# Branch gates of a hybrid decoder layer: 16 dense units, or seven block products with two of them beside the attention

## The chip, the core and the metric

The kernel runs on one core of one Trainium2 chip. The metric is device time in microseconds, the median of the runs; lower is better. The profile is of one execution, whose span goes from the first to the last instruction.

The engines by their names in the profile: PE is TensorE (matrix products), PEld its weight loads, DVE is VectorE (elementwise), ACT is ScalarE (elementwise, with tables for functions), POOL is GpSimd, SP is SyncE, which here issues every DMA in one queue. An engine works in the order of its own instructions; if one waits, those behind it wait too.

## What is computed

One layer over 1024 tokens of width 2048, in float32. Cut to what matters here:

```python
h = rmsnorm(x, g_pre)
u = h @ w_in                      # q, k, v of two kinds of attention, and two gates of 1024 columns
o_gla = rmsnorm(gla(...), g_gla_head) * silu(g_gate)
o_sb  = stick_breaking(...) * silu(s_gate)
mix = concat([o_gla, o_sb]) @ w_out
x = x + rmsnorm(mix, g_post)
x = x + sigmoid(x @ w_ple_gate + b_ple_gate) * (p @ w_ple_proj)
```

The change is about the 2048 gate columns of `w_in`: silu(g) times the attention's output.

## The kernel before

Everything is held transposed: features on the 128 partitions, tokens along the free dimension in two halves (`HALVES`) of 512. x is 16 tiles of 128 features per half. A float32 product is made of three matmuls in a rounded format: each operand is split (`split`) into `hi`, made by ScalarE, and `lo` = value - hi, made by VectorE, and hi*hi, lo*hi and hi*lo are summed in PSUM. The activations' halves are called `ah` and `al`, the weights' `hi` and `lo` (tiles of 128x512, read into `raw`, two buffers, split into four) or `wh` and `wl` (128x1024, read into `wr`, four buffers, split into three).

The stages, in order:

1. Units. `dense` makes 128 columns of h @ w_in for both halves: four weight tiles of 128x512 (`wload`), 16 x 2 x 3 = 96 matmuls. The 40 units of the attention come first. After each of its 16 steps, `step` lets the attention's generators (`jobs`) go on, so that the attention of one head stands among the units of the next. `rate` says how many pieces of a job one step lets through.
2. Gates. The 16 gate units of 128 columns. The first four (`EARLY_GATES`) are made while the last head's attention runs (`early_gate`), ten behind it from a pool `gates`, and the last two (`LATE_SOLO`), one half at a time, in the stage `mix`. For each gate the sum is multiplied with `rstd` (the norm of x), with its sigmoid and with the attention's output `o`, loaded from `o_d`; the product goes to `og_d`.
3. `w_out`, and after it `w_g` (w_ple_gate), each as a product of 2x2 blocks by 2x2 blocks with seven block products in place of eight (Winograd's form of Strassen's). A block is 512 tokens, 1024 rows and 1024 columns: `product` makes 128 of its columns with 24 matmuls, eight of them (j) one block product. The left factors are blocks and sums of blocks of the activations (A11, A12, A22, S1, S2, S3, S4), which are made and split in the background (`fill`, `sums_12`). The right factors are weight blocks or their sums, made for each j on VectorE (`t1`, `t2`, `t3`, `t4`); `t2` and `t3` go to memory (`t2_d`, `t3_d`) and are loaded again in later stages. `st_u` and `st_v` hold the running sums of the products. `add` and `sub` are lines 772 and 775.

A scheduler orders the instructions of each engine by priorities; `high_priority` (`ahead`, `soon`) moves the weights' loads and splits, and the additions to `u` and `v`, forward. A tile of a pool can only be loaded when what stood in its memory is done with.

In w_out's S2/S1 stage, each j loads three weight tiles, stores two and makes two products, with four `wr` buffers in all. In the code:

```python
b11, t1, t2 = (wload2(w_out[kh, nh, j]) for kh, nh in ((0, 0), (0, 1), (1, 1)))
sub(t1, t1, b11)
sub(t2, t1, t2)
w2, w1 = wsplit(t2), wsplit(t1)
add(b11, b11, t2)
dma(t2_d[j], t2)
dma(t3_d[j], b11)
```

Lines of before named below: 101 every matmul; 112 and 113 the two instructions of `split`; 129 the loads of `raw`; 310 to 331 and 579 to 605 the attention; 701 to 705 an early gate; 720 to 726 a gate of the pool `gates`; 761 the loads into `ar`; 779 the loads into `wr`; 915 the loads of the late gates' weights.

Of the kernel before, what the change touches and what calls it, by code (L numbers as in the profile page):

```python
# [36 lines left out]
def unit_offsets():  # L37
    offs = []
    for h in range(GLA_HEADS):
        offs += [OFF_GK + P * h, OFF_GQ + P * h, OFF_GV + 2 * P * h, OFF_GV + 2 * P * h + P]  # L40
    for h in range(SB_HEADS):
        offs += [OFF_SK + P * h, OFF_SQ + P * h, OFF_SV + P * h]
    offs += [OFF_GG + P * n for n in range(8)]
    offs += [OFF_SG + P * n for n in range(8)]
    return offs


N_UNITS = len(unit_offsets())
GATE0 = 40
EARLY_GATES = 4  # L50
LATE_SOLO = 2
# [8 lines left out]
RATE_BG = 0.5  # L60


@with_exitstack
def layer(ctx, tc, xT, w_in, w_lr, w_a2, b_a, g_pre, g_head, w_out, g_post,
# [15 lines left out]
    w_open = tc.tile_pool(name="w", bufs=4)  # L80
# [81 lines left out]
    urgent, jobs = deque(), deque()  # L162
    rate = [0.0, 0.0]

# [7 lines left out]
    def step():  # L172
        advance(urgent)
        rate[0] += rate[1]
        while rate[0] >= 1.0:
            rate[0] -= 1.0
            advance(jobs)
# [89 lines left out]
    with tc.tile_pool(name="att", bufs=1, reuse_waits="tile") as ap:  # L267
# [395 lines left out]

        rate[1] = RATE_GLA
        heads = [[{}, {}, {}, {}] for _ in range(GLA_HEADS)] + [[{}, {}, {}] for _ in range(SB_HEADS)]
        flat = [(h, i) for h, g in enumerate(heads) for i in range(len(g))]
        for u, (h, i) in enumerate(flat):
# [3 lines left out]
            elif i >= 2:  # L671
                ev = evac_turned(dst, 1 if h < GLA_HEADS else 2)
            else:
                ev = evac_plain(dst)
            if u < 2:
# [21 lines left out]
        def early_gate(n):  # L697
            def go(hf, p):
                gu, ol = at("u"), at("u")
                dma2(ol, part(o_d[hf][n // 2], n))  # L700
                V.tensor_tensor(gu, p, rstd[hf], op=ALU.mult)
                V.tensor_tensor(ol, ol, gu, op=ALU.mult)
                A.activation(gu, gu, AF.Sigmoid)
                V.tensor_tensor(ol, ol, gu, op=ALU.mult)
                dma2(part(og_d[hf][n // 2], n), ol)
            return go

        for n in range(EARLY_GATES):
            dense(U(GATE0 + n), x_act, HALVES, early_gate(n))
        while urgent or jobs:  # L710
            advance(urgent) or advance(jobs)
        own[0].__exit__(None, None, None)

    with tc.tile_pool(name="gates", bufs=1, reuse_waits="tile") as gp:
        def evac_gate(n):
            def go(hf, p):
                gu = gp.tile([P, HT], F32, tag="gu", name=nm("gu"), bufs=2)
                gs = gp.tile([P, HT], F32, tag="gs", name=nm("gs"), bufs=1)
                ol = gp.tile([P, HT], F32, tag="ol", name=nm("ol"), bufs=2)
                dma2(ol, part(o_d[hf][n // 2], n))  # L720
                V.tensor_tensor(gu, p, rstd[hf], op=ALU.mult)
                A.activation(gs, gu, AF.Sigmoid)
                V.tensor_tensor(ol, ol, gu, op=ALU.mult)
                o = gp.tile([P, HT], F32, tag="oB", name=nm("oB"), bufs=1)
                V.tensor_tensor(o, gs, ol, op=ALU.mult)
                dma2(part(og_d[hf][n // 2], n), o)
            return go
# [8 lines left out]

    slots = [[(1, kp) for kp in range(4)], [(1, kp) for kp in range(4, 8)], [(0, kp) for kp in range(4)]]
    with tc.tile_pool(name="mix", bufs=1, reuse_waits="tile") as mp:  # L740
        def mt(tag, bufs, n=W, dt=F32, name=None):
            return mp.tile([P, n], dt, tag=tag, name=nm(name or tag), bufs=bufs)

        for late in (("ev", 2), ("acc", 1), ("sq", 1), ("g", 1, HT), ("pr", 1, 256), ("ph", 1, 256), ("pl", 1, 256),
                     ("ar", 3)):
            mt(*late)
# [12 lines left out]
        def staged(src):  # L759
            t = mt("ar", 3)  # L760
            dma2(t, src)
            return t
# [27 lines left out]
        def product(a, w, mid=None, at=4, p=None, last=True):  # L790
            first = p is None
            p = p or ps("dn")
            hi, lo = w
            for k in range(8):
                sl = slice(k * P, (k + 1) * P)
                ah, al = a[k]
                mm(p, hi[:, sl], ah, first and k == 0, False)
                mm(p, lo[:, sl], ah, False, False)
                mm(p, hi[:, sl], al, False, last and k == 7)
# [15 lines left out]
        def fill(name, slot, make):  # L815
# [6 lines left out]
            sets[name] = parts(pairs)  # L822
# [11 lines left out]
        def sums_12(rows, s1, s2):  # L834
            for i in rows:
                a, b, c = staged(og_d[0][i]), staged(og_d[0][i + 4]), staged(og_d[1][i])
                add(a, a, b)
                sub(c, c, a)
                dma2(s2_d[i], c)
                yield 1  # L840
                s2.append(to_slot(1, i, c))
                yield 1
                if s1 is None:
                    dma2(s1_d[i], a)
                else:
                    s1.append(to_slot(2, i, a))
                yield 1

        def last_sums(s2):
            s1 = []  # L850
            for i in range(3):
                s1.append(to_slot(2, i, staged(s1_d[i])))
                yield 1
            yield from sums_12((3,), s1, s2)
# [4 lines left out]

        s1_d = drams("s1_d", 3)  # L860
# [43 lines left out]
        early = []  # L904
        for hf in (1, 0):
            if hf == 0:
                job(fill("A11", 0, plain(og_d[1])))
                job(sums_12(range(3), None, early))
            for n in range(KT - LATE_SOLO, KT):
                p = None  # L910
                for kh in HALVES:
                    with ahead():
                        raw = mt("wr", 4)
                        for q in range(2):
                            dma(part(raw, q), w_in[GATE0 + n, 2 * kh + q])
                        w = wsplit(raw)
                    p = product(x_act[hf][8 * kh:8 * kh + 8], w, p=p, last=kh == 1)
                with soon():
                    if n % 2 == 0:
                        z = mt("ev", 2)  # L920
                    V.tensor_tensor(part(z, n), p, rstd[hf], op=ALU.mult)
                    if n % 2:
                        o, g = staged(o_d[hf][n // 2]), mt("sq", 1)
                        A.activation(g, z, AF.Sigmoid)
                        V.tensor_tensor(z, z, o, op=ALU.mult)
                        V.tensor_tensor(z, z, g, op=ALU.mult)
                        dma2(og_d[hf][n // 2], z)
        drain()

        job(last_sums(early))  # L930
# [10 lines left out]
        job(fill("S3", 0, both(og_d[0], og_d[1], sub)))  # L941
        for j in range(8):
            with ahead():
# [5 lines left out]
                dma(t2_d[j], t2)  # L949
                dma(t3_d[j], b11)  # L950
# [8 lines left out]
        job(fill("A22", 1, plain(og_d[0][4:])))  # L959
        job(fill("A12", 2, plain(og_d[1][4:])))  # L960
        for j in range(8):
# [3 lines left out]
            with soon():  # L965
                if j % 2 == 0:
                    c = mt("ev", 2)
                add(part(c, j), p, v(j))
                add(u(j), p, u(j))
                if j % 2:  # L970
                    dma2(c_d[0][4 + j // 2], c)
# [252 lines left out]
```

## Time and profile before

| | us |
|---|---|
| median of 3 runs | 2149.65 (2147.41 to 2150.99) |
| the profiled execution | 2148.85 |
| its span | 2147.1 |
| TensorE's mean granted clock | 0.994 |
| stretch with four gates beside the last attention | 1078 to 1185 |
| ten gates alone | 1185 to 1412 |
| last two gates, then w_out and w_g | from 1423 |

All DMA moved 300 MB. A group row of the profile gives the line, engine and operation, the tiles written and read, the shape and the count, then busy time in us and the mean of one in ns, then the idle time of the engine just ahead of them and what ended it (`<-`). A row of the timeline gives start, duration, engine and the same names; in brackets the idle time ahead. The rows come in the prediction, where they are used.

### The profile page before, as it was taken

The page shows a single profiled execution, that of the slowest core. Times are in us where ns is not written, and L with a number is a line of the kernel's source. Part 1 is how long each engine was busy: PE and PEld are TensorE (multiplying, and loading weights), DVE is VectorE, ACT ScalarE, POOL GpSimd, SP SyncE. Part 2 cuts the span into 40 slices and gives each one's busy share as a digit, 9 for nine tenths or more (in the row PEclk, how much of TensorE's full clock was granted, in tenths as well). Part 3 has the DMA queues.
Part 4 walks back from the last instruction along what each step waited for, and adds up shares of the span by engine and source line. Part 5 has one row for each costly group of instructions (what it writes and reads, how often), then busy time and mean ns, then how long its engine had stood idle before and what let it go on. Part 6 is the DMA issues. An engine that isn't in the chain of part 4 may idle for free.

```text
span 2147.1 us, 26863 instructions
## 1 busy us (share of the span) xinstructions
PE 2111.7 (98%) x9904; PEld 1746.6 (81%) x9904; DVE 1372.7 (64%) x2147; ACT 831.1 (39%) x1347; POOL 106.7 (5%) x228
## 2 busy tenths in 40 slices
PE   9999999999999999999999999979999999999998
PEld 6788888888888888888888888868788888778787
DVE  8557676766666666666666232336777787886665
ACT  7333333333455454544544111123233443432332
POOL 3000000000101110110110000000000000000000
PEclk9999999999999999999999999989999999999999
DMA  6222221222233333333334333258887686786663
GB/s 205 73 54 56 59 61 59 55 60 55 62 86 89 75 89 88 89 81 78 93 102 120 94 98 98 87 174 311 312 319 251 219 312 205 271 286 219 223 206 123
DMA packets 215844, 300.38 MB, mean 140 GB/s; under 512 B 122913, under 2 KB 127905, under 8 KB 215713
## 3 DMA queue, kind: packets, MB, share of 16 engines
q1 hardware_dynamic: 215712, 298.67, 44.5%
q8 instruction: 77, 1.26, 0.2%
q14 instruction: 55, 0.44, 0.1%
HBM read 215.25 MB, written 56.10 MB: 126 GB/s over the span
## 4 chain that ended last, share of the span: by engine, by line
PE 77%; DMA 10%; DVE 8%; issue 2%; ACT 2%; SPq 0%; DVEq 0%; POOL 0%; ACTq 0%
PE dn L101 67%; PE z L101 5%; DMA wr<-w_g 3%; PE t L101 2%; PE o L101 2%; DVE wl L113 2%; DMA E<-X 1%; DMA ar<-h_d 1%; DMA ar<-og_d 1%; DMA wr<-w_out 1%; DVE ev L772 1%; DVE al L113 1%; DVE wr L772 1%; ACT ah L112 0%; DMA ar<-c_d 0%
## 5 line engine op out<-in xcount | busy, mean ns | idle before, releaser
L101 PE MATMUL dn<-ah,hi 128*128 128x512 f32 x1728 | 686.2, 397 | 0.2 <-ACT u L679 0.2
L101 PE MATMUL dn<-al,hi 128*128 128x512 f32 x1728 | 674.4, 390 | 0.9 <-DVE al L238 0.9
L101 PE MATMUL dn<-ah,lo 128*128 128x512 f32 x1728 | 673.8, 390 | 0.0
L101 PE MATMUL dn<-ah,wh 128*128 128x512 f32 x960 | 375.6, 391 | 11.0 <-ACT wh L112 11.0
L101 PEld LDWEIGHTS dn<-ah,hi 128*128 128x128 f32 x1728 | 325.0, 188 | 71.5 <-issue 3.6
L101 PEld LDWEIGHTS dn<-al,hi 128*128 128x128 f32 x1728 | 324.3, 188 | 72.2 <-DVE al L238 2.6
L101 PE MATMUL dn<-ah,wl 128*128 128x512 f32 x960 | 375.4, 391 | 3.5 <-DVE wl L113 3.5
L101 PE MATMUL dn<-al,wh 128*128 128x512 f32 x960 | 374.7, 391 | 0.0
L101 PEld LDWEIGHTS dn<-ah,lo 128*128 128x128 f32 x1728 | 325.2, 188 | 60.1
L112 ACT ACTIVATE hi<-raw 128x512 fp32r<-128x512 f32 x216 | 135.6, 628 | 304.5 <-PE dn L101 301.8
L113 DVE TENSOR_TENSOR lo<-raw,hi 128x512 fp32r<-128x512 f32 x216 | 150.3, 697 | 154.9 <-ACT hi L112 154.4
L101 PEld LDWEIGHTS dn<-ah,wh 128*128 128x128 f32 x960 | 181.4, 189 | 49.8 <-ACT wh L112 11.5
L101 PEld LDWEIGHTS dn<-ah,wl 128*128 128x128 f32 x960 | 181.5, 189 | 42.3 <-DVE wl L113 4.5
L101 PEld LDWEIGHTS dn<-al,wh 128*128 128x128 f32 x960 | 181.0, 189 | 37.5
L112 ACT ACTIVATE wh<-wr 128x1024 fp32r<-128x1024 f32 x120 | 126.0, 1055 | 186.7 <-PE dn L101 116.4
L113 DVE TENSOR_TENSOR wl<-wr,wh 128x1024 fp32r<-128x1024 f32 x120 | 145.8, 1218 | 18.3 <-ACT wh L112 17.8
L320 ACT ACTIVATE X<-E 128x256 uint16<-128x256 uint16 (+2 forms) x96 | 81.0, 844 | 128.5 <-DVE E L595 117.2
L590 DVE TENSOR_TENSOR_SCAN X<-X 128x128 f32<-128x128 f32 (+2 forms) x96 | 98.1, 1021 | 37.1 <-POOL X L584 24.6
L605 DVE COPY v<-E 128x512 uint16<-128x512 uint16 (+1 forms) x160 | 63.6, 430 | 59.5 <-DMA E<-X 50.2
L112 ACT ACTIVATE ah<-ar 128x1024 fp32r<-128x1024 f32 x48 | 50.9, 1061 | 105.8 <-DVE ar L775 50.8
L113 DVE TENSOR_TENSOR s<-v,s 128x512 fp32r<-128x512 f32 (+1 forms) x82 | 52.3, 637 | 48.3 <-ACT s L112 46.4
L112 ACT ACTIVATE s<-v 128x512 fp32r<-128x512 f32 (+1 forms) x82 | 47.9, 584 | 74.6 <-DVE v L605 43.3
(208 smaller groups left out, 2178.3 us busy)
## 6 DMA issues: line engine op xcount, KB each, us to landing
raw<-w_in SPq DMA_DIRECT2D x216, 256.0 KB, 2.7
wr<-w_g SPq DMA_DIRECT2D x64, 512.0 KB, 4.4
wr<-w_out SPq DMA_DIRECT2D x56, 512.0 KB, 4.8
ar<-og_d SPq DMA_DIRECT2D x36, 512.0 KB, 5.4
ar<-h_d SPq DMA_DIRECT2D x36, 512.0 KB, 4.8
xraw<-xT SPq DMA_DIRECT2D x32, 256.0 KB, 4.4
o_d<-o SPq DMA_DIRECT2D x32, 256.0 KB, 2.0
t_d<-wr SPq DMA_DIRECT2D x16, 512.0 KB, 3.2
```

What stands on the lines that cost most here:

```text
L101: PE.matmul(o, lhsT, rhs, start=start, stop=stop)
L112: A.activation(hi, src, AF.Copy)
L113: (eng or V).tensor_tensor(lo, src, f(hi), op=ALU.subtract)
L320: A.activation(pl.rearrange("p (two n) -> p two n", two=2), src.bitcast(U16)[:, :2 * n].rearrange("p (n two) -> p two n", two=2), AF.Copy)
L590: V.tensor_tensor_scan(rev, rev, rev, initial=kq[:, n:n + 1], op0=ALU.mult, op1=ALU.bypass)
L605: V.tensor_copy(to[:, :, :m, j], w[:, :, 2 * g:2 * g + m])
L772: V.tensor_tensor(dst, a, b, op=ALU.add)
```

## The change

The gates are made as the later two products are, by seven block products: the left factor is x times g_pre (not yet times `rstd`, which is multiplied in at the end), the right one `w_gate`, the gate columns as 2x2 blocks.

- `x_sums` makes the four sums S1 to S4 of x's blocks during the attention, from x in memory, 128x512 at a time in `u` tiles, and stores them (`sx_d`). It goes on once in 15 steps, and in the tail (from the first gate product on) `x_set` loads and splits S2 and S1 once in 4.
- Two block products, A11 by B11 and A12 by B21, are made by `small_product` beside the last attention, from `raw` tiles of 128x512: eight (j) of the first, whose results go to memory (`u1_d`, evacuated by ScalarE), and eight of the second, added to the first: gates 0 to 7 of the first half (`gate_11`). The last four of these (`LAST_11`) stand behind the attention and use the pool `mix`, which is opened ahead of them; the weights' pool is on the other side of the memory and stays open. The pool `gates` is gone.
- In the stage `mix`, S2/S1, A22, S3 and S4 follow as in the other two products; the gates of the second half come out in the S3 stage, the rest of the first half in the S4 stage (`gate`, two units at a time).
- `w_out` and `w_g` are made with the halves of the tokens exchanged: w_out's first product now takes og of the first half. `sums_12` makes S1 and S2 of w_out beside that product and splits both there; before, three of the four S1 tiles were stored and loaded again.
- `ar` has four buffers and not three, `ev` four and not two. The products of the per-layer embedding (`embed`) take turns on three PSUM tags.

The diff, cut:

```diff
-        for n in range(EARLY_GATES):
-            dense(U(GATE0 + n), x_act, HALVES, early_gate(n))
-        while urgent or jobs:
+        def small_product(a, src, evac):
+            p = ps("dn")
+            for q in range(2):
+                hi, lo = wload(part(src, q))
+                for kk in range(4):
+                    k = 4 * q + kk
+                    sl = slice(kk * P, (kk + 1) * P)
+                    ah, al = a[k]
+                    mm(p, hi[:, sl], ah, k == 0, False)
+                    mm(p, lo[:, sl], ah, False, False)
+                    mm(p, hi[:, sl], al, False, k == 7)
+                    if k % 2:
+                        step()
+            with tc.high_priority(offset=300):
+                evac(p)
+        def gate_11(j, new):
+            def go(p):
+                gu, ol = new(), new()
+                dma2(gu, part(u1_d[j // 2], j))
+                dma2(ol, part(o_d[0][j // 2], j))
+                V.tensor_tensor(gu, p, gu, op=ALU.add)
+                V.tensor_tensor(gu, gu, rstd[0], op=ALU.mult)
+                V.tensor_tensor(ol, ol, gu, op=ALU.mult)
+                A.activation(gu, gu, AF.Sigmoid)
+                V.tensor_tensor(ol, ol, gu, op=ALU.mult)
+                dma2(part(og_d[0][j // 2], j), ol)
+            return go
+        while beside:
+            advance(beside)
+        rate[1], pace[1] = RATE_TAIL, PACE_TAIL
+        beside.append(x_set("S2", 1))
+        for j in range(8):
+            small_product(x_act[0][:8], w_gate[0, 0, j], keep_u1(j))
+        while beside:
+            advance(beside)
+        beside.append(x_set("S1", 0))
+        for j in range(8 - LAST_11):
+            small_product(x_act[0][8:], w_gate[1, 0, j], gate_11(j, lambda: at("u")))
+        while urgent or jobs or beside:
...
-    with tc.tile_pool(name="gates", bufs=1, reuse_waits="tile") as gp:
...
-        for n in range(EARLY_GATES, KT - LATE_SOLO):
-            dense(U(GATE0 + n), x_act, HALVES, evac_gate(n))
+    for j in range(8 - LAST_11, 8):
+        small_product(x_act[0][8:], w_gate[1, 0, j], gate_11(j, lambda: part(mt("ar", 4), 0)))
...
-            for n in range(KT - LATE_SOLO, KT):
...
+        t2_d, t3_d = drams("g2_d", 8), drams("g3_d", 8)
+        for i in range(4):
+            dma2(st_u[i], u1_d[i])
+        for j in range(8):
+            with ahead():
+                b11, t1, t2 = (wload2(w_gate[kh, nh, j]) for kh, nh in ((0, 0), (0, 1), (1, 1)))
+                sub(t1, t1, b11)
+                sub(t2, t1, t2)
+                w2, w1 = wsplit(t2), wsplit(t1)
+                add(b11, b11, t2)
+                dma2(t2_d[j], t2)
+                dma2(t3_d[j], b11)
+            p = product(g_sets["S2"], w2)
+            with soon():
+                add(u(j), p, u(j))
+            p = product(g_sets["S1"], w1)
+            with soon():
+                add(v(j), p, u(j))
+        drain()
...
+            p = product(sets["S3"], w)
+            gate(j, 1, p, u(j))
+            gate(8 + j, 1, p, v(j))
...
+            p = product(sets["S4"], w)
+            gate(8 + j, 0, p, v(j))
...
+        job(sums_12())
```

Two places of the engines' orders. First VectorE beside the last attention. Before, among an early gate's rows (`lo` is a weight's split, `u` at lines 702 and 704 the gate, `v`, `s`, `X`, `E`, `eb` the attention):

```order
L113 TENSOR_TENSOR lo_10685<-raw_10683,hi_10684 128x512
L702 TENSOR_TENSOR u_10461<-u_10461,u_10460 128x512
L702 TENSOR_TENSOR u_10469<-u_10469,u_10468 128x512
L605 COPY v_10553<-E_2183_10415 128x2x2x128
L704 TENSOR_TENSOR u_10461<-u_10461,u_10460 128x512
L704 TENSOR_TENSOR u_10469<-u_10469,u_10468 128x512
L590 SCALAR_TENSOR_TENSOR X_10500<-X_10500 128x128
L113 TENSOR_TENSOR s_2216_10557<-v_10553,s_10556 128x512
L594 COPY eb_10510<-X_10500 128x1
L595 TENSOR_TENSOR E_10501<-E_10501,X_10500 128x128
```

Of the change, in the middle of the first block product (`al` is the split of a part of S2; a weight's split is line 112 now, the attention's rows are 593 to 608):

```order
L112 TENSOR_TENSOR al_10538<-u_10453,ah_10537 128x512
L608 COPY v_10606<-E_2199_10475 128x2x2x128
L112 TENSOR_TENSOR lo_10686<-raw_10684,hi_10685 128x512
L112 TENSOR_TENSOR s_2231_10610<-v_10606,s_10609 128x384
L112 TENSOR_TENSOR al_10538<-u_10541,ah_10537 128x512
L593 SCALAR_TENSOR_TENSOR X_10566<-X_10566 128x384
L112 TENSOR_TENSOR st_10658<-u_10132,st_10658 128x128
L598 TENSOR_TENSOR E_10567<-E_10567,X_10566 128x384
L112 TENSOR_TENSOR al_10727<-u_10633,ah_10726 128x512
L112 TENSOR_TENSOR lo_10745<-raw_10743,hi_10744 128x512
```

Between the attention's rows now stand splits of weights and of S2. From one weight split (`lo`) to the next are eight rows here; before they are fifteen.

Second SP's queue where the large weight tiles begin. Before, behind the last gates (`ol` is the attention's output, `oB` a finished gate):

```order
L720 DMA ol_12586<-o_d_0_687 128x512
L726 DMA og_d_1_711<-oB_12459 128x512
L720 DMA ol_12596<-o_d_1_695 128x512
L726 DMA og_d_0_703<-oB_12591 128x512
L726 DMA og_d_1_711<-oB_12601 128x512
L915 DMA wr_12684<-w_in 128x512 x2
L915 DMA wr_12716<-w_in 128x512 x2
```

Of the change (line 745 loads parts of S1, 786 stores a gate, 635 the attention's last output, 851 is `wload2`):

```order
L128 DMA raw_11483<-w_gate 128x512
L786 DMA og_d_0_702<-u_11283 128x512
L635 DMA o_d_1_700<-o_11335 128x512
L128 DMA raw_11501<-w_gate 128x512
L786 DMA og_d_0_702<-u_11352 128x512
L128 DMA raw_11530<-w_gate 128x512
L851 DMA wr_11664<-w_gate 128x1024
L128 DMA raw_11548<-w_gate 128x512
L851 DMA wr_11666<-w_gate 128x1024
L851 DMA wr_11668<-w_gate 128x1024
```

The first wr tile was loaded behind the last gate's store; now it is asked for ahead of the last raw tile, among the last four small products.

More of the change, by code (lines that the diff above doesn't have):

```diff
@@ L731, in layer @@
-    w_open.__exit__(None, None, None)
[L739 to L746, printed above, removed]
+    mp = ctx.enter_context(tc.tile_pool(name="mix", bufs=1, reuse_waits="tile"))
@@ L901, in stream @@
             yield 1
[L904 to L908, printed above, removed]
-            for n in range(KT - LATE_SOLO, KT):
[L910 to L927, printed above, removed]
@@ new lines, in layer @@
+        drain()
+        job(fill("S3", 1, plain(sx_d["S3"])))
+        job(fill("S4", 2, plain(sx_d["S4"])))
+        for j in range(8):
+            with ahead():
+                t4, t2 = wload2(w_gate[1, 0, j]), wload2(t2_d[j])
+                add(t4, t4, t2)
+                w = wsplit(t4)
+            p = product(x_act[1][8:], w)
+            with soon():
+                add(u(j), p, u(j))
+        drain()
+        for j in range(8):
+            with ahead():
+                w = wsplit(wload2(t3_d[j]))
+            p = product(sets["S3"], w)
+            gate(j, 1, p, u(j))
+            gate(8 + j, 1, p, v(j))
@@ L931, in layer @@
+        drain()
+        job(fill("A11", 0, plain(og_d[0])))
+        for j in range(8):
+            with ahead():
+                w = wsplit(wload2(w_gate[1, 1, j]))
+            p = product(sets["S4"], w)
+            gate(8 + j, 0, p, v(j))
+        drain()
+        st_u, st_v = state("h"), state("l")
+        job(sums_12())
         for j in range(8):
```

238 lines of the change are left out of this document (143 added, 95 removed).

## The prediction

> **What bounds the kernel now.** I read the page first, then TensorE's waits behind the attention, then the windows and the timeline around the gates. On the page TensorE is the engine without spare time:
>
> ```profile
> PE 2111.7 (98%) x9904; PEld 1746.6 (81%) x9904; DVE 1372.7 (64%) x2147; ACT 831.1 (39%) x1347; POOL 106.7 (5%) x228
> L101 PE MATMUL dn<-ah,hi 128*128 128x512 f32 x1728 | 686.2, 397 | 0.2 <-ACT u L679 0.2
> ```
>
> The 397 ns of one matmul is not what a matmul costs, since they overlap. What it costs is seen where nothing else runs, in the dense stretch of the chain of work behind the attention (start, us, what):
>
> ```profile
> 1184.90 226.48 PE dn L101 x999
> ```
>
> 226.48 us / 999 = **0.2267 us** per 128x512 matmul; a matmul that goes is worth this and not 0.397. The Trainium skill says the same in "Perfetto Trace Analysis", section "Identifying the Most-Contended Engine": busy time of matmuls is no measure of their cost. By busy time 192 matmuls would be 192 x 0.397 = 76 us; by the chain they are 43.5 us, and the sum goes by the chain.
>
> Where TensorE waits from the gates to the end of the kernel (who <- whom: us, times, longest):
>
> ```profile
> PE dn L101 <- ACT wh L112: 11.0, 1, 11.0
> PE z L101 <- DVE ev L1060: 4.2, 1, 4.2
> PE z L101 <- DVE pl L113: 3.6, 3, 1.8
> PE dn L101 <- DVE wl L113: 3.5, 2, 3.1
> ```
>
> The one wait of 11.0 us is at the end of the gates:
>
> ```profile
> 1411.66 0.39 PE L101 MATMUL dn<-al,hi 128*128 128x512 f32 x1
> ...
> 1416.67 0.69 DVE L725 TENSOR_TENSOR oB<-gs,ol 128x512 f32<-128x512 f32 x1 [2.10 <-DMA og_d<-oB]
> 1417.76 10.80 SPq L915 DMA_DIRECT2D wr<-w_in  x14
> 1421.97 1.06 ACT L112 ACTIVATE wh<-wr 128x1024 fp32r<-128x1024 f32 x1 [6.73 <-DMA wr<-w_in]
> ...
> 1423.08 0.80 PE L101 MATMUL dn<-ah,wh 128*128 128x512 f32 x1 [11.04 <-ACT wh L112]
> ...
> 1427.92 0.57 PE L101 MATMUL dn<-ah,wh 128*128 128x512 f32 x1
> ...
> 1428.33 0.39 PE L101 MATMUL dn<-ah,wl 128*128 128x512 f32 x1
> ```
>
> The first weights of the last stage are only asked for (SPq) when the last gate is written, because they stand in memory that the gates' pool held. Ten matmuls then start 0.43 us apart, at a lower granted clock. From 1411.66 to 1428.33 eleven steps take 16.67 us instead of 11 x 0.2267 = 2.49: **14.2 us** lost.
>
> **What is removed.** The gates were 16 units x 2 halves x 48 = 1536 matmuls; seven block products are 7 x 8 x 24 = 1344. The 192 that go are 192 x 0.2267 = **-43.5 us**. All of them are 128x512, and TensorE's order ahead of the gates stays, but for a few places where attention rows stand one step earlier or later.
>
> The gates' pool goes, and w_gate's first wr loads stand in SP's order ahead of the last raw load, among the last small products. The load after which they come waits for a split, which waits for a weight buffer that comes free 84 matmuls (19 us) before the first product with wr. From issue to landing such a load takes 4.8 us (page, part 6):
>
> ```profile
> wr<-w_out SPq DMA_DIRECT2D x56, 512.0 KB, 4.8
> ```
>
> With two differences and a split that is 4.8 + 2 x 1.22 + 1.06 + 1.22 = 9.5 us (VectorE's rows below, ScalarE's 1.06 above). So it should be hidden; bounds 0 and 14.2, I take 2 left over: **-14.2 + 2 us**.
>
> A third, smaller loss stands in w_out's S2/S1 stage:
>
> ```profile
> 1250.00:1300.00 50.00, 50.00 (x222) 41.38 (x222) 14.06 (x22) 8.00 (x13) 0.00 (x0) 1.00 0.27 90
> 1500.00:1550.00 50.00, 46.92 (x200) 38.15 (x199) 37.46 (x35) 15.78 (x18) 0.00 (x0) 0.97 0.89 316
> 1530.19 0.50 PE L101 MATMUL dn<-ah,wl 128*128 128x512 f32 x1 [3.08 <-DVE wl L113]
> ```
>
> (Columns of a window: us; busy and count of PE, PEld, DVE, ACT, POOL; clock; DMA share; GB/s.) 22 matmuls too few are 5.0 us: 3.1 of waiting, the rest lower clock behind it. Part of the cause goes, since S1 is no longer written to memory and loaded again there, but the four wr buffers with three loads and two stores per j stay. Bounds 0 and -5.0; I take **-2.5 us**.
>
> **What is added: VectorE beside the attention.** This term decides the size. In the stretch in which four gates run beside the last attention now:
>
> ```profile
> 1078.00:1184.90 106.90, 106.90 (x524) 90.48 (x523) 66.84 (x123) 47.77 (x90) 9.54 (x24) 1.00 0.39 109
> ```
>
> TensorE is never idle and VectorE is busy 66.84 of 106.90 us (0.625). What of it is gates and weights, and which of its waits are which (the groups of this window; last columns: busy, mean ns, idle before):
>
> ```profile
> L113 DVE TENSOR_TENSOR lo<-raw,hi 128x512 fp32r<-128x512 f32 x17 | 11.7, 686 | 12.1 <-ACT hi L112 12.1
> L605 DVE COPY v<-E 128x512 uint16<-128x512 uint16 x21 | 9.1, 458 | 5.2 <-DMA E<-X 4.9
> L113 DVE TENSOR_TENSOR s<-v,s 128x512 fp32r<-128x512 f32 x9 | 6.2, 686 | 7.8 <-ACT s L112 7.8
> L702 DVE TENSOR_TENSOR u<-u,u 128x512 f32<-128x512 f32 x6 | 4.0, 685 | 2.9 <-DMA u<-o_d 2.9
> L701 DVE TENSOR_TENSOR u<-dn,rstd 128x512 f32<-128x512 f32 x6 | 4.0, 683 | 1.8 <-PE dn L101 1.8
> L113 DVE TENSOR_TENSOR s<-v,s 128x384 fp32r<-128x384 f32 x5 | 2.8, 557 | 1.8 <-ACT s L112 1.7
> L704 DVE TENSOR_TENSOR u<-u,u 128x512 f32<-128x512 f32 x6 | 3.9, 683 | 0.0
> ```
>
> The attention itself is 66.84 - 11.7 - 4.0 - 4.0 - 3.9 = 43.2 us of VectorE, and 106.9 - 392 x 0.2267 = 18.0 us of TensorE (392 of the 524 are dn). The other prices:
>
> ```profile
> L113 DVE TENSOR_TENSOR lo<-raw,hi 128x512 fp32r<-128x512 f32 x216 | 150.3, 697 | 154.9 <-ACT hi L112 154.4
> L113 DVE TENSOR_TENSOR wl<-wr,wh 128x1024 fp32r<-128x1024 f32 x120 | 145.8, 1218 | 18.3 <-ACT wh L112 17.8
> L772 DVE TENSOR_TENSOR wr<-wr,wr 128x1024 f32<-128x1024 f32 x32 | 39.2, 1224 | 46.5 <-DMA wr<-w_g 32.9 <-DMA wr<-t_d 7.4 <-issue 6.0
> L897 DVE SCALAR_TENSOR_TENSOR ar<-ar,c,rstd 128x512 f32<-128x512 f32 x16 | 11.5, 746 | 7.0 <-DMA ar<-c_d 7.0
> ```
>
> A small product uses a split weight for one half of the tokens and not for two, so its splits are twice as dense. Twelve of them beside the attention: TensorE 288 x 0.2267 + 18.0 = 83.3 us. VectorE 43.2 + 24 splits x 0.697 + 16 splits of S2 and S1 x 0.697 + four gates x 4 x 0.684 = 43.2 + 16.7 + 11.2 + 10.9 = 82.0 us. The four late products with the first pair of weights: TensorE 96 x 0.2267 = 21.8; VectorE 8 x 0.697 + 10.9 + 3 x 1.224 + 2 x 1.218 = 22.6. Together **104.6 us of VectorE under 105.1 us of TensorE**. VectorE works in its order, so each wait in that order now moves TensorE, which waits for lo and s. It cannot gain: TensorE has no idle time there to give. The bounds are 0 and all of VectorE's waits in the window that do not come from its lead on weights: 106.9 - 66.84 - 12.1 = 28 us. I take the part which stays when VectorE is late: a copy v, ScalarE's split of it and the difference s follow each other closely, 7.8 + 1.8 = 9.6 us: **+10 us**.
>
> Behind them a pair j of the gates' S2/S1 stage costs VectorE 3 x 1.224 + 2 x 1.218 + 2 x 0.684 = 7.5 of TensorE's 10.9 us, so it gets its lead back. But the stage is built as w_out's, with four wr buffers, and starts without a lead: I take the 5.0 us that w_out's costs (bounds 0 and 10): **+5 us**.
>
> **What I cost at nothing.** S1 to S4 of x: 32 VectorE instructions, about 24 x 0.746 + 8 x 0.684 = 23.4 us over a thousand us, with 16 ACT copies. The attention has room:
>
> ```profile
> 1050.00:1100.00 50.00, 50.00 (x246) 42.26 (x245) 30.54 (x56) 25.47 (x45) 2.09 (x8) 1.00 0.33 85
> ```
>
> Without the cover it is 23 us at most. Its 64 transfers on SP stand between raw loads; a wait of theirs for a u buffer holds the raw loads behind it, which lead by four buffers of 24 matmuls. The gates' other stages: S3 costs VectorE 1.218 + 2 x 0.684 + 3 x 1.22 = 6.2 us per j against TensorE's 5.4, 6 us over in all, which three weight buffers (16 us) carry until S4, where it is 4.3. Exchanging the halves later changes names, not counts.
>
> **The sum**, against the profiled execution: 2147.1 - 43.5 - 14.2 + 2 - 2.5 + 10 + 5 = 2103.9 us of span; this execution took 1.75 us more than its span (2148.85), so 2105.7. The median of the runs shown, 2149.65, is 0.8 above it; I leave that out: **2106 us**.
>
> **The rivals.**
> *All is hidden.* VectorE reaches a full window in w_out's S2/S1 stage, so its waits could vanish (here us, busy VectorE, clock, DMA share, GB/s):
>
> ```profile
> 1540.00:1550.00 10.00, 10.00 (x11) 1.00 0.86 310
> ```
>
> No +10, +5, +2, and all 5.0 gained: 2147.1 - 43.5 - 14.2 - 5.0 + 1.75 = 2086. Against it speaks that the s chain is in the order itself. Chance 0.13.
>
> *DMA becomes the bound.* The new stages move, per 43.5 us, 24 transfers of 0.524 MB = 12.6 MB (A22: 16 loads of weights, 8 of S3 and S4; S3: 8 weights, 8 o, 8 og; w_out's first: 8 weights, 8 og, 8 stores), and 50 MB in the two double stages: 289 GB/s over some 350 us, S4 less. Now:
>
> ```profile
> 1450.00:1500.00 50.00, 50.00 (x223) 41.39 (x222) 30.50 (x28) 17.26 (x20) 0.00 (x0) 1.00 0.88 313
> 1550.00:1600.00 50.00, 50.00 (x223) 41.39 (x222) 39.58 (x39) 15.53 (x16) 0.00 (x0) 1.00 0.86 310
> ```
>
> 310 GB/s ran without a wait, which speaks against it; the 5.0 us at 316 GB/s for it. With one such loss in each of six stages: 2147.1 - 43.5 - 14.2 - 5.0 + 2 + 10 + 30 + 1.75 = 2128. Chance 0.12.
>
> *Slower: VectorE keeps its old share beside the attention.* If its waits grow with its work and it stays at 0.625, the 104.6 us take 167, 62 over TensorE's 105.1: 2105.7 - 10 + 62 = 2158. It decides below a share of 104.6 / (105.1 + 57) = 0.645 (over 2154). Against it: many of its present waits are lead, as the 12.1 us before lo. Chance 0.05, and 0.03 for a time beside no change.
>
> *The clock.* The 3.08 us wait above cost 5.0 us in all. If the 10 us come as three such waits they cost three times 1.9 more: 2111, inside the forecast. The Trainium skill, "TensorE: Matmul & The Clock Gate", section "What's actually happening", puts the idle window that halves the clock at about 3.4 us, by which waits of 3 us would cost nothing more; the 0.43 us steps behind this shorter wait say otherwise.
>
> **Chances.** Forecast 0.67 (own range 2094 to 2122), all hidden 0.13, DMA 0.12, slower 0.05, no change 0.03. The range of 8 in 10 goes from the hidden case to the DMA case with the late end of the tail's bound: 2086 to 2132. A measurement of this kernel tells about 0.2% from no change: faster 0.92, same 0.03, slower 0.05.
>
> **What would show it.** 9712 matmul records instead of 9904; the 11.0 us wait gone, with wr<-w_gate issued before the last small product; VectorE near 0.9 in the hundred us around the end of the attention, with TensorE waiting there for lo, s or wl. Wrong would be: no idle TensorE there (then 2086 to 2096), waits on wr from DMA all through the gates (then 2128), or VectorE under 0.65 (then slower).

## The result, and the profile after

| | before | after |
|---|---|---|
| median | 2148.53 us (4 runs, 2146.87 to 2150.99) | 2123.07 us (4 runs, 2120.21 to 2126.72) |
| profiled execution | 2148.85 | 2120.21 |
| its span | 2147.1 | 2118.3 |
| all DMA | 300 MB | 354 MB |

The ratio is 0.9882, 95% interval 0.9862 to 0.9901: faster, by 25 us (1.2%) and not by the 43 that were forecast. 2123 lies in the range of 2086 to 2132.

The engines' row on the page of after (lines are those of after: 100 is every matmul, 111 and 112 the split):

```profile
PE 2077.2 (98%) x9712; PEld 1712.5 (81%) x9712; DVE 1504.3 (71%) x2271; ACT 876.0 (41%) x1393; POOL 106.0 (5%) x228
```

9712 matmuls: the 192 are gone. The wait of 11.0 us for `wh` is gone too. In its place stand 13.3 us in four waits of TensorE for VectorE to take results out of PSUM (TensorE's waits from 1185 us on; who, for whom: us, times, longest):

```profile
PE dn L100 <- DVE ar L781: 8.2, 3, 4.8
PE dn L100 <- DVE st L844: 5.2, 1, 5.2
...
PE dn L100 <- DVE wl L112: 0.7, 1, 0.7
```

Line 781 is the addition in `gate_11` and 844 is `add`. Both read a `dn` bank of PSUM, and what waits is a matmul that wants that bank. Waiting for weights (`wl`) is down to 0.7 us.

To see where the time went I cut both executions at the same instructions. The last attention is cut from one of its value products on, which stands at 1092.42 us before and at 1095.47 us after:

```profile
1092.42 0.80 PE L101 MATMUL t<-s,u 128*128 128x256 f32 x6
```

```profile
1095.47 0.69 PE L100 MATMUL t<-s,u 128*128 128x256 f32 x5
```

From there to the end of the attention (us; busy and count of PE, PEld, DVE, ACT, POOL; clock; DMA share; GB/s), before:

```profile
1092.42:1184.90 92.48, 92.48 (x452) 78.23 (x451) 59.13 (x109) 42.87 (x81) 9.54 (x24) 1.00 0.41 114
```

and after, with the stretch behind it and the place of w_out's S2/S1 stage:

```profile
1095.47:1186.40 90.93, 83.30 (x392) 67.66 (x391) 64.62 (x119) 54.83 (x106) 8.81 (x23) 0.98 0.72 192
1186.40:1330.00 143.60, 130.27 (x548) 106.17 (x547) 101.66 (x111) 40.22 (x48) 0.00 (x0) 0.95 0.81 285
1500.00:1550.00 50.00, 49.25 (x217) 40.46 (x217) 37.55 (x37) 11.23 (x11) 0.00 (x0) 1.00 0.88 328
```

- Ahead of the cut: 3.05 us later than before.
- Beside the attention: 60 matmuls fewer are 13.6 us, but the stretch is only 1.55 us shorter. **12.0 us** are lost. VectorE is busy for 64.62 of 90.93 us, a share of 0.71.
- From the attention's end to 1330: 548 matmuls are 124.2 us of 143.6. **19.4 us** are lost, where before lost 14.2 at the end of its gates.
- w_out's S2/S1 stage: 5 matmuls too few in place of 22, so 1.1 us in place of 5.0.

-43.5 + 3.05 + 12.0 + 19.4 - 14.2 - 3.9 = -27.2 us, where the spans differ by -28.8; the other 1.6 us are spread over later stages.

The 19.4 us, row by row. These rows are picked from the timeline of after around the first products of the gates' S2/S1 stage; `...` parts one wait from the next (779 is a late gate's load of u1, 112 on `wl` the split of the weights, 998 the stores of `t3`, 989 the loads of u1 into `st_u`):

```profile
1202.18 0.43 SPq L779 DMA_DIRECT2D ar<-u_d  x1
1209.49 2.35 DVE L112 TENSOR_TENSOR wl<-wr,wh 128x1024 fp32r<-128x1024 f32 x2
1211.77 0.69 DVE L781 TENSOR_TENSOR ar<-dn,ar 128x512 f32<-128x512 f32 x1
1212.60 0.76 PE L100 MATMUL dn<-ah,wh 128*128 128x512 f32 x1 [3.10 <-DVE ar L781]
...
1230.81 0.32 SPq L998 DMA_DIRECT2D g_d<-wr  x1
1231.22 0.41 SPq L779 DMA_DIRECT2D ar<-u_d  x1
1235.10 0.69 DVE L781 TENSOR_TENSOR ar<-dn,ar 128x512 f32<-128x512 f32 x1 [0.81 <-DMA ar<-u_d]
1235.94 0.60 PE L100 MATMUL dn<-ah,wh 128*128 128x512 f32 x1 [4.84 <-DVE ar L781]
...
1242.99 0.32 SPq L998 DMA_DIRECT2D g_d<-wr  x1
1243.41 0.40 SPq L989 DMA_DIRECT2D st<-u_d  x1
1248.37 0.77 PE L100 MATMUL dn<-ah,wh 128*128 128x512 f32 x1 [5.15 <-DVE st L844]
```

The four `dn` banks hold the last gates' products, and each is free when line 781 has read it. Two things make that late. For the first of these gates it is VectorE's order: its u1 was asked for at 1202.18 and had landed 6.7 us later, but its addition stands behind the weight sums and two splits, which end at 1211.8, and VectorE is not idle ahead of it. TensorE waits 3.10 us. For the last gate it is the load of u1: SP issues it (1231.22) only behind a store that waits for VectorE's weight sum, and VectorE then stands 0.81 us until it has landed. TensorE waits 4.84 us. Such a load is the cause at 1243.41 too: the first loads for the S2 products' additions go out behind the stores of a later pair of weights, 31 us after the stage's first matmul (1212.60). This reading is a theory so far. Its rival is the one that the prediction had: weights without a lead.

### The profile page after: what moved, and what is told of

It reads as the page before. It is cut to its first block, busy times and chain, and to the rows that moved or that the text cites. A ratio compares the mean times of both kernels' runs of the same rounds, so it can differ in the third digit from the quotient of the medians.

```text
span 2118.3 us, 26833 instructions
## 1 busy us (share of the span) xinstructions
PE 2077.2 (98%) x9712; PEld 1712.5 (81%) x9712; DVE 1504.3 (71%) x2271; ACT 876.0 (41%) x1393; POOL 106.0 (5%) x228
## 4 chain that ended last, share of the span: by engine, by line
PE 73%; DMA 11%; DVE 10%; issue 3%; ACT 3%; SPq 0%; POOL 0%; DVEq 0%; ACTq 0%; POOLq 0%
PE dn L100 63%; PE z L100 5%; PE t L100 2%; PE o L100 2%; DVE wl L112 2%; DMA wr<-w_g 2%; DMA E<-X 1%; DMA ar<-og_d 1%; DMA wr<-w_gate 1%; DVE ev L844 1%; DMA wr<-w_out 1%; DMA ar<-h_d 1%; DMA xraw<-xT 1%; DVE al L112 1%; DVE wr L844 1%
## 5 line engine op out<-in xcount | busy, mean ns | idle before, releaser
L100 PE MATMUL dn<-ah,hi 128*128 128x512 f32 x1408 | 562.1, 399 | 0.2 <-ACT u L716 0.2
L100 PE MATMUL dn<-ah,lo 128*128 128x512 f32 x1408 | 549.9, 391 | 0.6 <-DVE lo L112 0.6
L100 PE MATMUL dn<-al,hi 128*128 128x512 f32 x1408 | 550.0, 391 | 0.4 <-DVE al L241 0.3
L100 PE MATMUL dn<-ah,wh 128*128 128x512 f32 x1216 | 476.0, 391 | 13.3 <-DVE ar L781 8.2
L100 PE MATMUL dn<-ah,wl 128*128 128x512 f32 x1216 | 475.6, 391 | 0.7 <-DVE wl L112 0.7
L100 PE MATMUL dn<-al,wh 128*128 128x512 f32 x1216 | 475.1, 391 | 0.1
L100 PEld LDWEIGHTS dn<-ah,hi 128*128 128x128 f32 x1408 | 265.3, 188 | 59.2 <-issue 2.8
L100 PEld LDWEIGHTS dn<-al,hi 128*128 128x128 f32 x1408 | 264.5, 188 | 59.0 <-DVE al L241 1.9
L100 PEld LDWEIGHTS dn<-ah,lo 128*128 128x128 f32 x1408 | 265.4, 189 | 48.7 <-DVE lo L112 1.1
L844 DVE TENSOR_TENSOR st<-dn,st 128x512 f32<-128x512 f32 x88 | 60.1, 686 | 47.7 <-PE dn L100 46.8
```

Of the source, the lines that this page charges most:

```text
L100: PE.matmul(o, lhsT, rhs, start=start, stop=stop)
L844: V.tensor_tensor(dst, a, b, op=ALU.add)
```

## The experiments

Each ran beside the kernel before on its own chip; ratios are to that.

**1. x_sums alone.** The kernel before, with `x_sums` and its steps and nothing else of the change.

```diff
+        pace[0] += 1
+        if pace[0] % pace[1] == 0:
+            advance(beside)
...
+            if u == 5:
+                beside.append(x_sums())
```

> The kernel before with the sums S1 to S4 of x made and stored during the attention and used by nobody (everything else as before, so the output is unchanged). The trace of the change enters the last attention 3.05 us later than before. If the sums cause that, this kernel is 3 us slower than before (2150 to 2154), with the loss ahead of 1095 us. If the prediction's price holds (hidden), it is within 1 us of before. If their VectorE time were exposed in full, it would be 23 us slower.

Measured: 2150.4 us against 2146.92, ratio 1.0017 (1.0005 to 1.0028). The last head's first 128x128 score product, before:

```profile
1097.23 0.22 PE L101 MATMUL z<-b,st 128*128 128x128 f32 x1
```

and here:

```profile
1102.94 0.22 PE L101 MATMUL z<-b,st 128*128 128x128 f32 x1
```

From there to the attention's end both take the same, 87.67 and 87.66 us. So the sums cost 5.7 us ahead of this point in this order, where the changed kernel was 3.05 us late: not nothing, and far from 23. Over the whole kernel they cost 3.5 us by the medians, as the first theory had it; in these two executions 2.4 us come back behind the attention.

**2. The last four gates' products leave PSUM by ScalarE.** `late_act`: a copy first, which needs no load, then the addition from the copy.

```diff
+    def gate_freed(j):
+        def go(p):
+            t, g = part(freed[j // 2 % 2], j), mt("ar", 4)
+            A.activation(t, p, AF.Copy)
+            gate_11(j, iter((part(g, 0), part(g, 1))).__next__)(t)
+        return go
...
-        small_product(x_act[0][8:], w_gate[1, 0, j], gate_11(j, lambda: part(mt("ar", 4), 0)))
+        small_product(x_act[0][8:], w_gate[1, 0, j], gate_freed(j))
```

> The last four gates' products are copied out of PSUM by ScalarE at once, so that no PSUM bank waits for VectorE's addition or for the load of u1; all else as in the change, four 0.6 us copies more on ScalarE. Theory PSUM (the late additions hold the four banks and TensorE stands still for them): the waits of 3.1, 0.2 and 4.8 us and the slow clock behind them go, 10 to 16 us faster than the change (about 2109). Theory lead (the first wr tile is asked for only 9.6 us ahead of the last small product's end, and four wr buffers give a pair of weights only every 10.5 to 12 us): TensorE then waits for wh or wl at nearly the same times, 0 to 4 us faster (2119 to 2123).

Measured: 2117.6 us, ratio 0.9868 (0.9851 to 0.9884). The waits for line 781 are gone, and one wait takes their place (853 is `add` here, 1007 a store of `t3`, 998 the loads of u1 into `st_u`, 112 the split of the third pair's first weights):

```profile
1229.55 1.23 DVE L112 TENSOR_TENSOR wl<-wr,wh 128x1024 fp32r<-128x1024 f32 x1
...
1240.50 0.32 SPq L1007 DMA_DIRECT2D g_d<-wr  x1
1240.92 0.40 SPq L998 DMA_DIRECT2D st<-u_d  x1
...
1245.46 1.89 DVE L853 TENSOR_TENSOR st<-dn,st 128x512 f32<-128x512 f32 x3 [1.82 <-DMA st<-u_d]
1246.30 0.76 PE L100 MATMUL dn<-ah,wh 128*128 128x512 f32 x1 [14.61 <-DVE st L853]
```

TensorE made products until all four banks were full and then stood for 14.61 us, until the load issued at 1240.92 let VectorE add. Banks, not weights, stop it: the fifth product needs the first weights of the third pair, and these were split by 1230.78 us, before the fourth product's last matmul (1231.31). The loss to 1330 is 17.6 us. The time, 5.5 us under the change, is what neither theory had forecast: the waits for line 781 went, as the theory of PSUM said, but the wait for line 844 grew by 9.5 us.

**3. Six late gates.** `last6`: more work between the attention and the stage.

```diff
-LAST_11 = 4
+LAST_11 = 6
```

> Six of the second product's eight parts stand behind the attention and not four (LAST_11 = 6), so 29 matmuls (6.6 us) more lie between the attention's end and the first S2 product. Theory lead: wr is asked for as much earlier, and the loss between the attention's end and 100 us behind it falls from 19 to about 12 us. Theory PSUM: six late additions hold the banks, the loss stays at 19 or grows. Beside the attention ten products stand and not twelve; if VectorE and the attention's own pace set the time there, that stretch gets shorter by less than the matmuls moved out of it, and its loss grows from 11 to 13 to 17 us, so that the total stays within 4 us of the change.

Measured: 2116.38 us, ratio 0.9858 (0.9843 to 0.9872). The first wr load goes out at 1186.62 us, 13 us earlier than in after, and still there is one wait of 9.38 us for line 781; the loss to 1330 is 12.1 us. The 12.1 us are what the theory of the lead had forecast, and the time, 6.7 us under the change, is more than the 4 us of the other. But the mechanism is not the lead's: no wait for `wh` or `wl` stands there in either kernel, and with a lead longer by 13 us the wait for a bank stays, longer than any in after. It is now a late gate's own product that waits, for an addition that stands in VectorE's order behind the second pair's weight sums. Why the loss as a whole fell, this run alone does not tell.

**4. The loads of u1 early.** `st_first`: the four loads into `st_u` get a higher priority and stand in SP's order right behind the first pair's stores. `banks` is this and the copies of 2 together.

```diff
-        for i in range(4):
-            dma2(st_u[i], u1_d[i])
+        with tc.high_priority(offset=1500):
+            for i in range(4):
+                dma2(st_u[i], u1_d[i])
```

> The early loads of u1 alone, beside the changed kernel's own order of additions. If PSUM banks set it: only the wait for the S2/S1 products' additions goes (5.15 us in the changed kernel), the waits for the last four gates' additions (3.1 + 0.2 + 4.8 us) stay; loss 13 to 16 us in place of 19.4, 2116 to 2120 us. If the lead of the weights sets it: loss 18 us or more, 2121 to 2124 us.

> The last four gates' products are copied out of PSUM by ScalarE, and the four loads of u1 that the first S2 and S1 additions need are asked for right behind the first stored weight differences. If PSUM banks held by late loads set the start of the S2/S1 products: the 14.6 us wait of late_act goes to under 4 us, the loss from the attention's end to 1330 falls from 17.6 to 6 to 9 us, the time to 2105 to 2110 us. If the lead of the S2/S1 weights sets it: waits for w splits take the place of the 14.6 us wait, the loss stays at 14 us or more, the time at 2113 to 2118 us.

Measured: `st_first` 2107.3 us, ratio 0.981 (0.9794 to 0.9826); `banks` 2106.72 us, 0.9806 (0.9789 to 0.9824). TensorE's waits from the attention's end to 1330, `st_first`:

```profile
PE dn L100 <- DVE ar L781: 4.8, 2, 4.0
PE dn L100 <- DVE st L844: 0.9, 1, 0.9
```

and `banks`:

```profile
PE dn L100 <- ACT wh L111: 2.4, 3, 1.6
PE dn L100 <- DVE wl L112: 1.1, 2, 0.8
```

Four DMA issues moved by some 33 us give back 15 us, 11.6 of them between the attention's end and 1330. That is more than I had expected of `st_first` (2116 to 2120): I had counted only the wait for line 844, which falls from 5.15 to 0.9 us, but banks that come free there also spare the later waits that were put down to line 781 (0.24 and 4.84 us, now one of 0.83). The wait at the stage's first matmul stays, 3.99 us in place of 3.10: early loads do not change VectorE's order, in which this addition stands behind weight sums and splits. In `banks` the copies by ScalarE take it away. `banks` also shows what the rival theory is worth: without any wait for a bank, 3.5 us of waiting for weights remain, and a loss of 6.3 us.

**5. Both, with six late gates.** `banks6` is `banks` with `LAST_11 = 6`, `st6` is `st_first` with it, without the copies.

> Both edits, with six of the eight second-part gate products at the S2/S1 start in place of four. If banks and lead each bind in part: TensorE has 7.3 us more ready work there, loss from the attention's end to 1330 of 3 to 7 us, 2100 to 2107 us. If SP's queue in order (loads behind stores that wait for VectorE) still sets it: loss stays at last6's 12 us, 2112 to 2117 us.

> st_first with six in place of four of the second-part gate products behind the attention, without the copies by ScalarE. If the four PSUM banks are held by the gates' additions wherever these stand behind others on VectorE: waits of 6 to 10 us for the additions stay at the S2/S1 start, 2107 to 2112 us. If the early loads of u1 alone free the banks in time: loss from the attention's end to 1330 of 1 to 4 us, 2104 to 2107 us as banks6.

Measured: `banks6` 2105.82 us, ratio 0.9806 (0.9789 to 0.9823); `st6` 2116.73 us, 0.9858 (0.9839 to 0.9878). In `banks6` TensorE is hardly ever idle behind the attention:

```profile
1183.40:1330.00 146.60, 145.82 (x643) 120.39 (x643) 110.48 (x122) 45.66 (x56) 0.00 (x0) 1.00 0.90 312
```

643 matmuls are 145.8 us: 0.8 us lost, at 312 GB/s, less than the 3 to 7 that I had expected. `st6` has a wait of 8.38 us for line 781 again, as the first theory had it, though its time lies 4.7 us above that theory's range. With six gates behind the attention the copies are needed, with four they add nothing that these runs can tell.

| | attention's end | matmuls to 1330 | lost, us |
|---|---|---|---|
| after | 1186.40 | 548 | 19.4 |
| late_act | 1185.40 | 560 | 17.6 |
| last6 | 1182.30 | 598 | 12.1 |
| st6 | 1184.65 | 592 | 11.1 |
| st_first | 1185.70 | 602 | 7.8 |
| banks | 1187.20 | 602 | 6.3 |
| banks6 | 1183.40 | 643 | 0.8 |

(lost = 1330 - end - matmuls x 0.2267.) `banks6` loses 5.5 us less here than `banks`, but its median is only 0.9 us lower: it has two gates fewer beside the attention, and loses 4.8 us more there (345 matmuls in 84.1 us, where `banks` has 374 in 85.9). That is the second question.

**6. What costs 12 us beside the attention?** Four kernels change how the sets S2 and S1 come in (`x_set`). `tail_noload` splits each set's eight parts from one loaded part; `tail_halfsplit` keeps the loads and splits every second part (a copy of eight columns stands for the other splits); `tail_none` has one load and one split for each set; `tail_ahead` leaves nothing out and only asks for each part one step earlier:

```diff
+            late = load(0)
             for k in range(8):
-                t = at("u")
-                dma2(t, part(sx_d[name][k // 2], k))
+                t, late = late, load(k + 1) if k < 7 else None
                 yield 1
```

> S2 and S1 beside the attention are split from one loaded part each, in place of eight (14 loads of 256 KB fewer; as many splits; the sums in the gates' S2 and S1 products are therefore not the right ones). Theory loads (ScalarE and VectorE stand in order behind these loads, which stand in SP's order among the attention's transposes): the loss beside the attention falls from 11.2 to 5 us or less. Theory load of VectorE, or pace (the attention's pieces are made 1.2 times as densely and wait for each other): it stays at 9 to 12 us, and the total within 3 us of the change.

> Beside the last attention all loads are kept, but every second token part takes the split of the part before, so VectorE's and ScalarE's split work halves there (the products with those parts then use other tokens than the reference). If the loads on which ScalarE and VectorE stand set the loss of 11.4 us beside the last attention: it stays at 10 to 12 us, 2119 to 2123 us. If the split work sets it: it falls to 5 to 8 us, 2115 to 2119 us.

> The changed kernel, but each S2/S1 token part is asked for one step earlier, so that its load has a step more before ScalarE's split of it. If late loads hold ScalarE and VectorE up beside the last attention: ScalarE's 9.3 us of waits for S1 and S2 parts go, the loss there falls from about 12 to 7 to 9 us (from z 128x128 to the attention's end 83 to 85 us in place of 87.4), 2117 to 2120 us. If the split work sets it: the waits move to other things, the loss stays at 11 to 13 us, 2121 to 2125 us.

> The changed kernel with one load and one split for each of the S2 and S1 sets in place of eight, so that all products with a set use its first token part. If loads and splits of the two sets together make the loss beside the last attention: the attention ends 6 us or more before 1186.4, loss from z 128x128 to its end of 12 us falls to 2 to 5. If the order of attention, gate additions and weight splits on ScalarE and VectorE sets it: loss stays at 7 to 9 us, as with half the splits alone or no loads alone. The time behind that is not predicted by either, since the S2/S1 start keeps its waits; some 2108 to 2118 us.

Measured from the 128x128 score product to the attention's end, one execution each, in which each of these has the same 374 matmuls:

| | us | median of runs | ratio |
|---|---|---|---|
| after | 87.42 | 2123.07 | 0.9882 (0.9862 to 0.9901) |
| tail_none | 86.52 | 2114.4 | 0.9854 (0.9836 to 0.9873) |
| tail_ahead | 83.43 | 2116.13 | 0.9857 (0.9834 to 0.9879) |
| tail_noload | 83.24 | 2116.21 | 0.9852 (0.9832 to 0.9871) |
| tail_halfsplit | 82.57 | 2119.2 | 0.9867 (0.9852 to 0.9882) |
| st_first, banks (not changed here) | 86.71, 85.82 | | |

Without waits these 374 would take some 75.4 us (87.67 before, less 54 x 0.2267), so the losses are 12.0 us in after, 11.1 in `tail_none` and 7.1 to 8.0 in the other three. Each partial change gained 4 to 5 us, which by itself would have made either theory look right. The kernel that takes away nearly all loads and splits gained 0.9, and neither of its forecasts (2 to 5 us of loss, 7 to 9) came. It waits about as long as after does, 7.0 us and 7.3. TensorE's waits from 1095 to 1187 in after:

```profile
PE t L100 <- ACT s L111: 2.4, 3, 1.3
PE z L100 <- ACT E L583: 2.0, 1, 2.0
PE z L100 <- ACT st L111: 1.7, 1, 1.7
PE dn L100 <- DVE lo L112: 0.6, 1, 0.6
PE t L100 <- DVE s L112: 0.6, 2, 0.5
```

and from 1099 to 1187 in `tail_none`, with its window:

```profile
PE t L100 <- ACT s L111: 3.8, 2, 2.5
PE t L100 <- DVE s L112: 1.7, 3, 1.1
PE z L100 <- ACT E L583: 0.8, 1, 0.8
PE dn L100 <- DVE lo L112: 0.7, 1, 0.7
```

```profile
1098.99:1185.51 86.52, 79.47 (x374) 64.92 (x373) 58.70 (x108) 47.79 (x94) 9.82 (x23) 0.98 0.60 167
```

All but 0.6 and 0.7 us are waits for the attention's own tiles: `s` (the values' weights, split), `E` (the sigmoid that reads the scores), `st` (the queries, split). So neither the sets' loads nor their splits are what the loss is made of, though the order in which they stand moves it by 4 us. Before, with 60 matmuls more in the same stretch, none of these waits appeared. That the attention's own steps now have too little beside them to hide behind fits all of this; it was argued from the names of the waits, and not tried by itself. Why one order of the same work is 4 us better than another also stays open.

**7. The best version.** `banks6_ahead` is `banks6` with the loads of `tail_ahead`.

> banks6 with the same earlier loads. By late loads: 2 to 4 us below banks6, 2101 to 2104 us. By split work: 2104 to 2107 us.

Measured: **2103.04 us** (2102.56 to 2103.95), ratio 0.9794 (0.9776 to 0.9813), 45 us under the kernel before and about 20 under the change. TensorE waits for `dn` once between the attention's end and 1340:

```profile
PE dn L100 <- DVE st L858: 0.8, 1, 0.8
```

It lies 2.8 us below `banks6` in another set of runs, and the two intervals overlap: that the earlier loads help on top of the rest is not settled.

## Why the prediction was right, and where it was not

Direction and range held; the time was 17 us over the forecast. By its steps, as spans of the profiled execution, the fastest of the four (forecast 2103.9, measured 2118.3):

- **192 x 0.2267 = -43.5 us**: held. 9712 matmuls, and in the stretches without waits they stand at this distance.
- **The wait of 14.2 us at the gates' end, less 2 left over**: the old wait went. The first wr load was not asked for 19 us ahead but 9.6 (issued at 1199.72, the last small product ended at 1209.34). That is as long as the 9.5 us worked out for load, differences and split; `banks`, where nothing else stops TensorE, shows 3.5 us of waits for weights. The step's size was about right, though its lead was not. One reading in it was loose: of the ten steps behind the old wait the first two took 1.26 us (with 0.46 of waiting for `wl`) and 0.59, and the other eight are those of 0.43; the 14.2 us stand.
- **"The stage is built as w_out's, with four wr buffers, and starts without a lead", +5 (0 to 10)**: this is the step that failed. With the +2 above it had 7 us for what cost 19.4. The prediction followed the weights into the stage and did not follow the results out of it: it never listed what the additions at lines 781 and 844 need, where SP issues those loads, nor where the additions stand in VectorE's order. In SP's order one load of u1 stands behind each pair's stores until 1243.41, and there are four banks to wait in. `st_first` (four issues moved, 15 us back) and `banks6` (0.8 us lost) show it. w_out's own stage was no model, since its first product's results are still in `st_u`, and this one has to load them.
- **VectorE beside the attention, +10 (0 to 28)**: 12.0 measured, by another way than named. VectorE was to be full, with 104.6 us of work under 105.1 of TensorE. In the stretch of the sixteen small products, 1094.11 to 1209.34 us, it did 80.7 us in 115.2, a share of 0.70. The late gates' 10.9 us and the first pair's two splits stood behind that stretch, where TensorE then waited for the additions among them, and the attention took some 8 us less than the 43.2 that were read from the window from 1078 on, which holds more of it. And taking 14 splits and 14 loads away (`tail_none`) gave back 0.9 us. The 9.6 us of waits for a copy v, its split and the difference s are nearer to what the waits name, but the agreement in size is no proof.
- **x_sums at nothing, 23 at most**: 3.05 ahead of the cut in the change, 5.7 there alone and 3.5 over that whole kernel; small but not nothing.
- **w_out's S2/S1, -2.5 (0 to -5.0)**: -3.9.
- **Rivals.** All hidden (2086) fell with the first waits; that DMA is the bound fell too, since in `banks6` 312 GB/s ran over 146.6 us with 0.8 us lost, and that in a wait for VectorE. Slower fell: a share of 0.70 is above its point of 0.645, and the 104.6 us of work were not there. On the clock: three long waits came, with 5.5 us on top of them where three times 1.9 had been reckoned, but in the gates' stage and not beside the attention.
- **Its signs.** The 9712 records came, the wait of 11.0 us went, and `wr` was asked for ahead of the last small product. VectorE near 0.9 around the end of the attention did not come (0.75 from 1136.4 to 1236.4). Beside the attention TensorE waited 3.6 us for `s` and `lo`, as named, and 3.7 us for `E` and `st`.

The terms' errors: +3.05 +2.0 +12.4 -1.4 and -1.65 in later stages make +14.4 us, the difference of the spans.

## What to carry to other kernels

Where a new stage follows another at once, follow the results as closely as the weights: for each evacuation list what else it reads, where in its queue that load is issued, and where in its engine's order the evacuation itself stands, since PSUM banks that wait for a late load, or for an engine that is busy with something else, stop TensorE as surely as missing weights. A small load issued behind stores that wait for computed data is late by that computation; moving four such issues was worth 15 us here, more than half of what the whole change had brought. And a part of a theory that is taken away and gains something has not proved it: take away all of it too, and see whether the gain grows.

## What the runs showed of the hardware

Each of the three long waits of TensorE cost 1.5 to 2.3 us on top of itself. The timeline of after, behind the wait of 4.84 us:

```profile
1236.34 0.63 PE L100 MATMUL dn<-ah,wl 128*128 128x512 f32 x1
1236.77 0.63 PE L100 MATMUL dn<-al,wh 128*128 128x512 f32 x1
...
1239.65 0.39 PE L100 MATMUL dn<-ah,wh 128*128 128x512 f32 x1
1239.88 0.39 PE L100 MATMUL dn<-ah,wl 128*128 128x512 f32 x1
```

The matmuls start 0.43 us apart until 1239.33 and 0.23 us apart from 1239.65 on: nine steps from 1235.94 take 3.71 us in place of 2.04. Behind the waits of 3.10 and 5.15 us it is 1.5 and 2.3 us more. The three make 5.5 of the 19.4 us, so that 18.8 us of the loss are these waits (13.3 us with one of 0.24) and their echo. The wait of 14.61 us in `late_act` cost no more on top: eight steps behind it take 3.49 us in place of 1.81. The granted clock is low there: just behind the wait of 5.15 us, in ten us without any wait, it was 0.84, with 38 matmuls in place of some 44 (after):

```profile
1250.00:1260.00 10.00, 10.00 (x38) 8.09 (x38) 5.61 (x6) 1.06 (x1) 0.00 (x0) 0.84 0.91 338
```

The slow stretch need not begin at once: in `tail_none`, behind a wait of 3.76 us, the matmuls start 0.24 us apart for 1.5 us, and only then 0.43 us apart:

```profile
1230.38 0.47 PE L100 MATMUL dn<-ah,wh 128*128 128x512 f32 x1 [3.76 <-DVE ar L779]
...
1231.61 0.39 PE L100 MATMUL dn<-al,wh 128*128 128x512 f32 x1
1231.84 0.59 PE L100 MATMUL dn<-ah,wh 128*128 128x512 f32 x1
1232.23 0.63 PE L100 MATMUL dn<-ah,wl 128*128 128x512 f32 x1
```
